# A reciprocal on another engine, an early tile for one set of matrices, and x loaded inside the gated unit: one step of a two-layer S5 and pooling backbone

## The chip, the core and the metric

The kernel runs on one core of a Trainium2 chip. The metric is the device time of one execution in microseconds (us). The core has five engines that run beside each other and wait for one another by semaphores: TensorE (PE in the rows; PEld is its weight load), VectorE (DVE), ScalarE (ACT), GpSimd (POOL) and SyncE (SP), which here does nothing but issue DMA transfers. ACT and POOL issue some transfers too. Each engine works off its own instructions strictly in the order in which they stand, so an instruction that waits holds up all that stands behind it.

## The reference

Two token streams go through the same two layers: a context of 128 tokens and a latent grid of 1024 tokens, both 1024 wide, in fp32. A layer is a token mixer, a LayerNorm, a SwiGLU of inner width 2816 and a second LayerNorm, each with modulation vectors that come from a conditioning vector. Layer 0 mixes with a bidirectional state-space scan, layer 1 by pooling over windows. Cut to layer 0, where the change lies:

```
def s5_mixer(h, ...):
    u = h.reshape(bsz, seq_len, 64, 16)
    y = u * d_skip
    for d in range(2):                       # forward, backward
        s_re, s_im, f_re, f_im = s5_scan(u, ..., reverse=(d == 1))
        y = y + (einsum(s_re, c_re[d]) - einsum(s_im, c_im[d]))
    y = gelu(y.reshape(bsz, seq_len, D_MODEL))
    val, gate = split(y @ glu_w + glu_b, 2)  # the gated unit
    return val * sigmoid(gate), ...

oc, fin_re, fin_im = s5_mixer(hc, ..., zeros, zeros)                 # context
ol, _, _ = s5_mixer(hl, ..., state_ssm_re, state_ssm_im)             # latents
xc = layer_norm(ALPHA * xc + g1c * oc, ...)
xl = layer_norm(ALPHA * xl + g1l * ol, ...)
fc = swiglu(modulate(xc, sh2c, sc2c), w_gate[i], w_up[i], w_down[i])
fl = swiglu(modulate(xl, sh2l, sc2l), w_gate[i], w_up[i], w_down[i])
```

`layer_norm` subtracts the mean over the 1024 channels and multiplies by `rsqrt(var + 1e-5)`.

## The kernel before

The scan is cut into chunks of 8 tokens: 128 chunks of the latents, 16 of the context. Within a chunk everything is a matrix product, between the chunks a recurrence is stepped.

**Tables (0 to about 176 us).** `ssm` loads parameters, and for each of eight blocks of 128 channels (`kt`, 8 groups of 16 channels) `ssm_u` transposes the input into `u`, `ssm_in` and `ssm_v` make the chunk inputs of the scan, `Z[0]` (forward) and `Z[1]` (backward), and `ssm_tables` makes two sets of matrices and writes them to DRAM: `kd[kt]` (the in-chunk matrices) and `mo[kt]` (from state to output, 1 MB). The adaLN weights (`adaw`) are loaded and multiplied beside it.

**Scan.** `scan_step` (lines 477 and 482) takes one chunk of both directions forward on VectorE: two products into `stt`, four sums into `Z`. First 15 steps for the context, then 127 for the latents (`ssm_scan_lat`).

**Context output.** `ssm_y_ctx` multiplies, for each `kt`, `u` by `mk` (L645) and the states by `mo` (L648), both loaded by `load_mo` (L589: eight pieces of `kd`, and L595: `mo`), applies a gelu and transposes (L659) into `xmc`. `load_mo` keeps the last four `mk` (4 buffers) and the last two `mo` (2 buffers). Then `ctx0a` runs the context's gated unit (`glu`, weights in `raw`) and its LayerNorm (`ln`), while the latent scan runs. With `scanning` set, `elem` gives GpSimd for the context's elementwise work; `ln_stats` takes the square root on ScalarE (L981), `nc.vector.reciprocal` on VectorE (L982) and refines the result by one Newton step (`stt`, on GpSimd here).

**Latent output.** `ssm_y` copies the states of a `kt` into `sd` (L626 ACT, L628 POOL, L630 DVE; 3 buffers), multiplies by `mk` and `mo` (L674, L677), applies a gelu on ScalarE (`yl`, L680) and writes `yd[kt]` to DRAM by POOL (L683). The order is 6, 7, 4, 5, 0, 1, 2, 3, so that `mk` of 4 to 7 and `mo` of 6 and 7 are still there. Beside it run the first 15 of the 22 steps of the context's SwiGLU (`ctx0b`, `ffn` L841): each is two weights of 0.5 MB through `raw`, which has three buffers for all users, and PE products into `psc`, which has two.

**Gated unit of the latents.** `yd` is read back as `yr` (L1187, two buffers, issued by POOL) and split by ScalarE and VectorE into a high and a low part (`xm`, `xn`, L821 and L822). `load_x` brings x in eight tiles of 128 tokens (`xr`, through `raw`), transposes them on PE (`px`, L421) and copies them on ScalarE (L422). Then `glu` runs for the first half A and the second half B of the latents; each of 8 values of `m` takes two weights through `raw`, split into `wh` and `wl`, and 48 products of 128x512. The remaining steps of the context's SwiGLU run between them with weights in `rc`.

After that both halves go through the SwiGLU, and layer 1 follows.

**What sets the order.** Every instruction is recorded in program order, and `TileContext(schedule_with_timeline_sim=True)` lets a scheduler put each engine's instructions, and the DMAs of each queue, in an order of its own, by durations that it assumes. So a change of one line can move instructions at many places. Buffers of a pool are handed on in turn; a transfer into a buffer waits on its queue until the last reader is through.

Of the kernel before, what the change touches and what calls it, by code (L numbers as in the profile page):

```python
# [41 lines left out]
class Kernel:  # L42
# [366 lines left out]

    def load_x(self):  # L410

        nc = self.nc
        xs = self.I["x_sample"].rearrange("o n d -> (o n) d")
        for q in range(8):
            xp = self.raw.tile([128, 1024], F32, tag="raw", name=f"xr{q}")
# [114 lines left out]
    def ssm_tables(self, tmp, kt, si):  # L530
# [50 lines left out]
        nc.scalar.dma_start(self.kd[kt].rearrange("g h m -> (g h) m"), ks.rearrange("p j h -> p (j h)"))  # L581

    def load_mo(self, tmp, kt):


        if kt not in self.mks[-4:]:
            m = tmp.tile([128, 8, 128], F32, tag="mk", name="mk", bufs=4)
            for s in range(8):
                self.nc.sync.dma_start(m[16 * s:16 * s + 16],  # L589
                                       self.kd[kt].rearrange("g h m -> h g m")[:, :, 16 * s:16 * s + 128])  # L590
            self.mks.append(kt)
            self.held["m", kt] = m
        if kt not in self.mos[-2:]:
            mo = tmp.tile([128, 2048], F32, tag="mo", name="mo", bufs=2)
            self.nc.sync.dma_start(mo, self.mo[kt])  # L595
            self.mos.append(kt)
            self.held["o", kt] = mo
        return (self.held["m", kt],
                self.held["o", kt].rearrange("p (d x g m) -> p d x g m", d=2, x=2, g=4))
# [88 lines left out]
    def ssm(self):  # L688
# [8 lines left out]
        with R("sst") as tmp:  # L697
            with R("ad0", "left") as ad:
                arow = self.ssm_params(pp, tmp, ad)
            self.ssm_modvec(pp, tmp, arow)  # L700
            self.ssm_dskip(pp, tmp)
        self.u = left.enter_context(R("ssmu", "left")).tile([128, G, NCH], F32, name="u")
        self.adp = self.rawc = None
# [4 lines left out]
        with R("ssu") as tmp:  # L708
            for kt in range(KT):
# [5 lines left out]
                for d in range(2):  # L715
                    self.ssm_in(si, d, kt, 4)
                self.ssm_tables(so, kt, si)
            while self.late:
                self.ssm_v()
# [8 lines left out]
        with R("ssy") as tmp:  # L728
            self.mks, self.mos, self.held = [], [], {}
            self.scanning = True  # L730
# [9 lines left out]
            self.ssm_scan_lat()  # L740
            for kt in (6, 7, 4, 5, 0, 1, 2, 3):
                self.ssm_y(tmp, kt)
# [141 lines left out]

    def glu(self, b, x, fill=iter(()), vx=lambda a: a, vs=lambda a: a):
        nc, I = self.nc, self.I
        gw = I["ssm_glu_w"][0].rearrange("(k p) m -> p k m", p=128)
        for m in range(8):
# [3 lines left out]
            nc.scalar.activation(sg, pg, AF.Sigmoid, bias=self.glu_b[:, 1, m:m + 1])  # L892
            self.stt(b, sg, pv, self.glu_b[:, 0, m:m + 1], sg, OP.add, OP.mult, self.glu_b[:, 0, m:m + 1])
            self.stt(b, vx(b.x[:, m, :]), vs(sg), self.gate[0, 0][:, b.i, m:m + 1], vx(b.x[:, m, :]),
                     OP.mult, OP.add)
# [59 lines left out]
    def ln_stats(self, b):  # L955
# [25 lines left out]
        nc.scalar.activation(q, pv, AF.Sqrt, bias=self.eps if b.split else self.epsc[:, 0:1])  # L981
        nc.vector.reciprocal(r, q)  # L982
        self.stt(b, q, pv, LN_EPS / (ALPHA * ALPHA), r, OP.add, OP.mult, self.epsc[:, 0:1])
# [163 lines left out]
    def build(self):  # L1147
        tc, nc = self.tc, self.nc
        with ExitStack() as st:
# [16 lines left out]
            self.gate, self.lnm = {}, {}  # L1166
            self.scanning = False
            self.ident = self.cp.tile([128, 128], F32, name="ident")
            make_identity(nc, self.ident)
# [11 lines left out]
            with tc.tile_pool(name="xm1", bufs=1) as xmp:  # L1181
                xm = [xmp.tile([128, 8, 512], F32R, name=f"xm{q}") for q in range(2)]
                with tc.tile_pool(name="glup", bufs=1) as tmp:
                    xm2 = [tmp.tile([128, 8, 512], F32R, name=f"xn{q}") for q in range(2)]
                    for k in range(8):
# [4 lines left out]
                        for q, x in enumerate((xm, xm2)):  # L1190
                            self.split_into(tok(x[0]), tok(x[1]), yv[:, ::-1, 64 * q:64 * q + 64])
                    self.load_x()
                    with tc.tile_pool(name="rawc", bufs=1) as self.rawc:
                        self.glu(A, xm, fill)
                        self.glu(B, xm2, fill)
# [120 lines left out]
```

## Time and profile before

| | us |
|---|---|
| median of 3 runs (2436.50 to 2446.79) | 2441.52 |
| the profiled execution | 2435.49 |
| its span, first to last instruction | 2433.7 |
| PE busy in it | 2243.9 (92%) |
| DVE busy | 1274.6 (52%) |
| ACT busy | 926.1 (38%) |
| POOL busy | 267.2 (11%) |

A row of the profile names the source line, the engine, the operation and the tiles (written tile first, buffer numbers left out), with partitions x elements. Times in the timeline views count from the first instruction. The span is 1.8 us shorter than the execution's own time. A step of the program order ("ffn", say) often stands in the trace as two records, since an fp32 product takes two passes. DMA shares are the mean busy share of 16 DMA engines.

### The profile page before, as it was taken

The page shows a single profiled execution, that of the slowest core. Times are in us where ns is not written, and L with a number is a line of the kernel's source. Part 1 is how long each engine was busy: PE and PEld are TensorE (multiplying, and loading weights), DVE is VectorE, ACT ScalarE, POOL GpSimd, SP SyncE. Part 2 cuts the span into 40 slices and gives each one's busy share as a digit, 9 for nine tenths or more (in the row PEclk, how much of TensorE's full clock was granted, in tenths as well). Part 3 has the DMA queues.
Part 4 walks back from the last instruction along what each step waited for, and adds up shares of the span by engine and source line. Part 5 has one row for each costly group of instructions (what it writes and reads, how often), then busy time and mean ns, then how long its engine had stood idle before and what let it go on. Part 6 is the DMA issues. An engine that isn't in the chain of part 4 may idle for free.

```text
span 2433.7 us, 33343 instructions
## 1 busy us (share of the span) xinstructions
PE 2243.9 (92%) x13105; PEld 1874.0 (77%) x13105; DVE 1274.6 (52%) x2421; ACT 926.1 (38%) x1377; POOL 267.2 (11%) x337
## 2 busy tenths in 40 slices
PE   4886768699999999999999999889999999999996
PEld 2655768588887777788888888777788888888996
DVE  6779684254546222456322775778422456422476
ACT  3763225343225222544322543226322443322464
POOL 4931236300010000100000010002000100000000
PEclk7995889799999999999999999999999999999998
DMA  7877559754554554423333225764333223333452
GB/s 226 247 236 199 156 150 271 207 156 145 160 166 153 160 187 160 169 96 95 96 99 100 96 96 161 231 193 135 104 100 99 96 95 96 95 96 100 143 200 104
DMA packets 458012, 357.22 MB, mean 147 GB/s; under 512 B 14960, under 2 KB 405888, under 8 KB 455808
## 3 DMA queue, kind: packets, MB, share of 16 engines
q1 hardware_dynamic: 451920, 340.91, 46.6%
q0 software_dynamic: 3200, 8.39, 1.2%
q10 hardware_dynamic: 2736, 5.80, 0.6%
q8 instruction: 103, 1.69, 0.3%
q14 instruction: 53, 0.43, 0.1%
HBM read 336.58 MB, written 18.35 MB: 146 GB/s over the span
## 4 chain that ended last, share of the span: by engine, by line
PE 79%; DMA 13%; DVE 3%; issue 2%; ACT 2%; POOL 1%; SPq 1%; ACTq 0%; DVEq 0%; POOLq 0%
PE ffn L837 13%; PE ffn L839 13%; PE ffn L838 13%; PE dn L838 6%; PE dn L837 6%; PE dn L839 6%; PE ffn L841 3%; PE dn L841 3%; DMA adaw<-ada_w 2%; PE glu L838 2%; PE glu L839 2%; PE glu L837 2%; DMA raw<-ffn_w_gate 2%; DMA raw<-ffn_w_down 1%; DMA raw<-ssm_glu_w 1%
## 5 line engine op out<-in xcount | busy, mean ns | idle before, releaser
L821 ACT ACTIVATE wh<-raw 128x1024 fp32r<-128x1024 f32 (+1 forms) x326 | 342.1, 1050 | 936.6 <-PE ffn L838 613.0
L822 DVE TENSOR_TENSOR wl<-raw,wh 128x1024 fp32r<-128x1024 f32 (+1 forms) x326 | 394.7, 1211 | 512.2 <-ACT wh L821 504.8
L838 PE MATMUL dn<-hkl,wh 128*128 128x512 f32 (+1 forms) x880 | 304.5, 348 | 0.3 <-DVE hkl L822 0.3
L839 PE MATMUL dn<-hkh,wl 128*128 128x512 f32 (+1 forms) x880 | 303.0, 347 | 0.0
L837 PE MATMUL ffn<-xp,wh 128*128 128x512 f32 x704 | 274.9, 391 | 2.2 <-ACT wh L821 2.2
L837 PE MATMUL ffn<-xm,wh 128*128 128x512 f32 x704 | 274.4, 391 | 1.3 <-ACT xm L821 0.7
L839 PE MATMUL ffn<-xp,wl 128*128 128x512 f32 x704 | 275.2, 391 | 0.2 <-DVE wl L822 0.2
L839 PE MATMUL ffn<-xm,wl 128*128 128x512 f32 x704 | 274.8, 391 | 0.0
L838 PE MATMUL ffn<-xm,wh 128*128 128x512 f32 x704 | 274.8, 390 | 0.0
L838 PE MATMUL ffn<-xp,wh 128*128 128x512 f32 x704 | 274.6, 391 | 0.0
L837 PE MATMUL dn<-hkh,wh 128*128 128x512 f32 (+1 forms) x880 | 262.5, 348 | 0.9 <-ACT hkh L821 0.9
L910 DVE TENSOR_TENSOR h<-ffn,sg 128x512 f32<-128x512 f32 x88 | 60.7, 689 | 245.2 <-PE ffn L839 245.1
L838 PEld LDWEIGHTS dn<-hkl,wh 128*128 128x128 f32 x880 | 166.6, 189 | 21.0 <-DVE hkl L822 0.5
L839 PEld LDWEIGHTS dn<-hkh,wl 128*128 128x128 f32 x880 | 166.5, 189 | 20.5
L837 PEld LDWEIGHTS dn<-hkh,wh 128*128 128x128 f32 x880 | 163.3, 189 | 23.3 <-ACT hkh L821 1.7
L841 PE MATMUL ffn<-xmc,raw 128*128 128x128 f32 x1184 | 149.6, 282 | 31.0 <-DMA raw<-ffn_w_gate 10.3
L841 PEld LDWEIGHTS ffn<-xmc,raw 128*128 128x128 f32 x1184 | 141.9, 196 | 40.3 <-DMA raw<-ffn_w_up 11.1
L837 PEld LDWEIGHTS ffn<-xm,wh 128*128 128x128 f32 x704 | 132.1, 188 | 33.1 <-issue 3.8
L837 PEld LDWEIGHTS ffn<-xp,wh 128*128 128x128 f32 x704 | 132.5, 188 | 30.4 <-ACT wh L821 2.5
L839 PEld LDWEIGHTS ffn<-xp,wl 128*128 128x128 f32 x704 | 132.5, 188 | 29.0 <-DVE wl L822 0.9
L839 PEld LDWEIGHTS ffn<-xm,wl 128*128 128x128 f32 x704 | 132.2, 188 | 29.0 <-issue 1.5
L838 PEld LDWEIGHTS ffn<-xp,wh 128*128 128x128 f32 x704 | 132.5, 188 | 28.1 <-issue 0.5
(331 smaller groups left out, 3308.0 us busy)
## 6 DMA issues: line engine op xcount, KB each, us to landing
raw<-ffn_w_down SPq DMA_DIRECT2D x126, 512.0 KB
raw<-ffn_w_gate SPq DMA_DIRECT2D x125, 512.0 KB
raw<-ffn_w_up SPq DMA_DIRECT2D x125, 512.0 KB
adaw<-ada_w SPq DMA_DIRECT2D x96, 512.0 KB
raw<-ssm_glu_w SPq DMA_DIRECT2D x48, 512.0 KB
mo<-mo SPq DMA_DIRECT2D x14, 1024.0 KB
rc<-ffn_w_down SPq DMA_DIRECT2D x40, 256.0 KB
mo<-otab SPq DMA_DIRECT2D x32, 256.0 KB
```

What stands on the lines that cost most here:

```text
L821: nc.scalar.activation(h, src, AF.Copy)
L822: nc.vector.tensor_tensor(l, src, h.bitcast(F32), op=OP.subtract)
L837: nc.tensor.matmul(ps, wh, xh, start=start, stop=False)
L838: nc.tensor.matmul(ps, wh, xl, start=False, stop=False)
L839: nc.tensor.matmul(ps, wl, xh, start=False, stop=stop)
L841: nc.tensor.matmul(ps, w[0], x[0], start=start, stop=stop)
L910: v.tensor_tensor(h[:, f, :], self.in_sb(b, v, pu), sg, op=OP.mult)
```

## The change

Four edits. `ln_stats` takes the reciprocal on the engine that `elem` gives: on VectorE as before, on GpSimd as a power with exponent -1, read from a new one-column tile `minus`. This concerns the context's first LayerNorm alone, the only one that runs with `scanning` set. `mk0`, the in-chunk matrices of block 0, gets a tile of its own, loaded while the tables of block 3 are made; the ring of `mk` has three buffers instead of four, and the latent blocks come in the order 6, 7, 5, 0, 1, 2, 3, 4. `load_x` takes a list of tiles and is called inside `glu` of half A, for tiles 0 to 3 at `m = 0` and for 4 to 7 at `m = 3`, instead of ahead of it. The memset of `minus` is added at the start.

```diff
--- before.py
+++ after.py
@@ -407,11 +407,11 @@
                 nc.scalar.activation(self.XC.rearrange("p k (c t) -> p t k c", t=8)[:, 4 * half + t4],
                                      px[:, 128 * t4:128 * t4 + 128].rearrange("p (k c) -> p k c", c=16), AF.Copy)
 
-    def load_x(self):
+    def load_x(self, qs):
 
         nc = self.nc
         xs = self.I["x_sample"].rearrange("o n d -> (o n) d")
-        for q in range(8):
+        for q in qs:
             xp = self.raw.tile([128, 1024], F32, tag="raw", name=f"xr{q}")
             nc.sync.dma_start(xp, xs[128 * q:128 * q + 128, :])
             for kh in range(2):
@@ -580,14 +580,17 @@
                                            kp[po, 224 + 16 * gp:240 + 16 * gp], op0=OP.mult, op1=OP.add)
         nc.scalar.dma_start(self.kd[kt].rearrange("g h m -> (g h) m"), ks.rearrange("p j h -> p (j h)"))
 
+    def load_mk(self, m, kt):
+        for s in range(8):
+            self.nc.sync.dma_start(m[16 * s:16 * s + 16],
+                                   self.kd[kt].rearrange("g h m -> h g m")[:, :, 16 * s:16 * s + 128])
+
     def load_mo(self, tmp, kt):
 
 
-        if kt not in self.mks[-4:]:
-            m = tmp.tile([128, 8, 128], F32, tag="mk", name="mk", bufs=4)
-            for s in range(8):
-                self.nc.sync.dma_start(m[16 * s:16 * s + 16],
-                                       self.kd[kt].rearrange("g h m -> h g m")[:, :, 16 * s:16 * s + 128])
+        if kt not in self.mks[-3:] and kt:
+            m = tmp.tile([128, 8, 128], F32, tag="mk", name="mk", bufs=3)
+            self.load_mk(m, kt)
             self.mks.append(kt)
             self.held["m", kt] = m
         if kt not in self.mos[-2:]:
@@ -699,6 +702,8 @@
                 arow = self.ssm_params(pp, tmp, ad)
             self.ssm_modvec(pp, tmp, arow)
             self.ssm_dskip(pp, tmp)
+        mk0 = left.enter_context(R("ssmk", "left")).tile([128, 8, 128], F32, name="mk0")
+        self.held = {("m", 0): mk0}
         self.u = left.enter_context(R("ssmu", "left")).tile([128, G, NCH], F32, name="u")
         self.adp = self.rawc = None
         self.Z = []
@@ -715,6 +720,8 @@
                 for d in range(2):
                     self.ssm_in(si, d, kt, 4)
                 self.ssm_tables(so, kt, si)
+                if kt == 3:
+                    self.load_mk(mk0, 0)
             while self.late:
                 self.ssm_v()
         self.ssm_scan_ctx(si)
@@ -726,7 +733,7 @@
         self.open_ctx(cblk)
         self.open_hc(cblk)
         with R("ssy") as tmp:
-            self.mks, self.mos, self.held = [], [], {}
+            self.mks, self.mos = [], []
             self.scanning = True
             self.yb = [tmp.tile([128, 8, 8, 16], F32, tag="yl", name=f"yb{q}", bufs=2) for q in range(2)]
             for q in range(2):
@@ -738,7 +745,7 @@
             self.drain(fill)
             self.ctx0a()
             self.ssm_scan_lat()
-            for kt in (6, 7, 4, 5, 0, 1, 2, 3):
+            for kt in (6, 7, 5, 0, 1, 2, 3, 4):
                 self.ssm_y(tmp, kt)
         left.close()
         self.cright = right
@@ -882,7 +889,7 @@
             v.tensor_scalar(t, x, s, None, op0=op0)
         v.tensor_tensor(out, t, y, op=op1)
 
-    def glu(self, b, x, fill=iter(()), vx=lambda a: a, vs=lambda a: a):
+    def glu(self, b, x, fill=iter(()), vx=lambda a: a, vs=lambda a: a, hooks={}):
         nc, I = self.nc, self.I
         gw = I["ssm_glu_w"][0].rearrange("(k p) m -> p k m", p=128)
         for m in range(8):
@@ -891,6 +898,7 @@
             sg = b.tmp.tile([128, b.n], F32, tag="sg" + b.tg, name="sg", bufs=2)
             nc.scalar.activation(sg, pg, AF.Sigmoid, bias=self.glu_b[:, 1, m:m + 1])
             self.stt(b, sg, pv, self.glu_b[:, 0, m:m + 1], sg, OP.add, OP.mult, self.glu_b[:, 0, m:m + 1])
+            self.load_x(hooks.get(m, ()))
             self.stt(b, vx(b.x[:, m, :]), vs(sg), self.gate[0, 0][:, b.i, m:m + 1], vx(b.x[:, m, :]),
                      OP.mult, OP.add)
             next(fill, None)
@@ -979,7 +987,10 @@
         r = b.tmp.tile([128, n], F32, tag="lr" + b.tg, name="lr", bufs=1)
         q = b.tmp.tile([128, n], F32, tag="lq" + b.tg, name="lq", bufs=1)
         nc.scalar.activation(q, pv, AF.Sqrt, bias=self.eps if b.split else self.epsc[:, 0:1])
-        nc.vector.reciprocal(r, q)
+        if v is nc.vector:
+            v.reciprocal(r, q)
+        else:
+            v.tensor_tensor(r, q, self.minus.to_broadcast([128, n]), op=OP.pow)
         self.stt(b, q, pv, LN_EPS / (ALPHA * ALPHA), r, OP.add, OP.mult, self.epsc[:, 0:1])
         self.stt(b, q, q, -0.5, r, OP.mult, OP.mult)
         self.stt(b, r, q, 1.5, r, OP.add, OP.mult)
@@ -1165,6 +1176,8 @@
             self.XC = P("xcres").tile([128, 8, 128], F32, name="XC")
             self.gate, self.lnm = {}, {}
             self.scanning = False
+            self.minus = self.cp.tile([128, 1], F32, name="minus")
+            nc.vector.memset(self.minus, -1.0)
             self.ident = self.cp.tile([128, 128], F32, name="ident")
             make_identity(nc, self.ident)
             self.ssm()
@@ -1189,9 +1202,8 @@
                         tok = lambda a: a[:, k].rearrange("p (c t) -> p t c", t=8)
                         for q, x in enumerate((xm, xm2)):
                             self.split_into(tok(x[0]), tok(x[1]), yv[:, ::-1, 64 * q:64 * q + 64])
-                    self.load_x()
                     with tc.tile_pool(name="rawc", bufs=1) as self.rawc:
-                        self.glu(A, xm, fill)
+                        self.glu(A, xm, fill, hooks={0: range(4), 3: range(4, 8)})
                         self.glu(B, xm2, fill)
                         self.drain(fill)
                     self.rawc = None
```

The scheduler moves much more than that. Three places follow; first before, then after. (Line numbers grow by up to 13.)

On DVE, in the middle of the latent scan, the reciprocal stood between two sums of one scan step (`stt` and `Z` are the two directions' tiles, `lr` and `lq` the LayerNorm's):

```order
L477 TENSOR_TENSOR stt_364<-rm,Z_566 128x128
L482 TENSOR_TENSOR Z_562<-stt_363,Z_562 128x64
L482 TENSOR_TENSOR Z_566<-stt_364,Z_566 128x64
L482 TENSOR_TENSOR Z_562<-stt_363,Z_562 128x64
L982 RECIPROCAL lr<-lq 128x128
L482 TENSOR_TENSOR Z_566<-stt_364,Z_566 128x64
L477 TENSOR_TENSOR stt_363<-rm,Z_562 128x128
```

Now it stands on POOL between the sum of squares and the Newton step of the same LayerNorm, and DVE has nothing but scan steps there:

```order
L984 TENSOR_TENSOR sq<-sq 128x256 x3
L985 TENSOR_TENSOR sq<-sq 128x128
L993 TENSOR_TENSOR lr<-lq,minus 128x128
L890 TENSOR_TENSOR lq<-st,lr 128x128
L889 TENSOR_SCALAR st<-lq 128x128
L890 TENSOR_TENSOR lq<-st,lr 128x128
L889 TENSOR_SCALAR st<-lq 128x128
L890 TENSOR_TENSOR lr<-st,lr 128x128
```

The instruction has gone from one in-order engine to another, and stays at its place in the LayerNorm's chain.

On SP, at the end of the latent blocks, where x and the first weights of the gated unit are loaded (`xr` x, `mo` a block's state matrices, `mk` its in-chunk matrices):

```order
L589 DMA mk<-kd_97 16x8x128 x7
L416 DMA xr_4828<-x_sample 128x1024
L416 DMA xr_4842<-x_sample 128x1024
L416 DMA xr_4856<-x_sample 128x1024
L595 DMA mo<-mo_88 128x2048
L595 DMA mo<-mo_89 128x2048
L416 DMA xr_4870<-x_sample 128x1024
L416 DMA xr_4884<-x_sample 128x1024
L416 DMA xr_4898<-x_sample 128x1024
L416 DMA xr_4912<-x_sample 128x1024
L416 DMA xr_4926<-x_sample 128x1024
L830 DMA raw<-ssm_glu_w 128x8x128 x5
```

Now:

```order
L598 DMA mo<-mo_90 128x2048
L837 DMA raw<-ffn_w_gate 128x8x128
L837 DMA raw<-ffn_w_up 128x8x128
L837 DMA raw<-ffn_w_gate 128x8x128
L837 DMA raw<-ffn_w_up 128x8x128
L837 DMA raw<-ssm_glu_w 128x8x128 x2
L416 DMA xr_4902<-x_sample 128x1024
L416 DMA xr_4916<-x_sample 128x1024
L416 DMA xr_4930<-x_sample 128x1024
L1294 DMA rc<-ffn_w_gate 128x4x128 x2
L1294 DMA rc<-ffn_w_up 128x4x128 x2
L1294 DMA rc<-ffn_w_gate 128x4x128 x2
```

The loads of x stand behind the first two weights of the gated unit, and the context's last weights of these 15 steps behind the last `mo`: before, the first `mo` of the latent blocks stood behind 22 of the 30 `raw` weights, now behind 9, and the last one behind 26.

On DVE, at the end of the scan (`hc` is the product that ends a step of the context's SwiGLU, `sd` the copies of a latent block):

```order
L477 TENSOR_TENSOR stt_363<-rm,Z_562 128x128
L910 TENSOR_TENSOR hc<-ffn,sg 128x128
L477 TENSOR_TENSOR stt_364<-rm,Z_566 128x128
L482 TENSOR_TENSOR Z_562<-stt_363,Z_562 128x64
L482 TENSOR_TENSOR Z_566<-stt_364,Z_566 128x64
L482 TENSOR_TENSOR Z_562<-stt_363,Z_562 128x64
L482 TENSOR_TENSOR Z_566<-stt_364,Z_566 128x64
L630 COPY sd<-Z_562 64x512
```

Now:

```order
L477 TENSOR_TENSOR stt_366<-rm,Z_572 128x128
L477 TENSOR_TENSOR stt_365<-rm,Z_568 128x128
L482 TENSOR_TENSOR Z_572<-stt_366,Z_572 128x64
L482 TENSOR_TENSOR Z_568<-stt_365,Z_568 128x64
L482 TENSOR_TENSOR Z_572<-stt_366,Z_572 128x64
L482 TENSOR_TENSOR Z_568<-stt_365,Z_568 128x64
L477 TENSOR_TENSOR stt_366<-rm,Z_572 128x128
L633 COPY sd<-Z_568 64x512
```

The products `hc` that stood inside the scan are gone from it; the first one on DVE now stands behind the copies of four latent blocks.

## Rows read from the trace of the kernel before

**Rows 1.** Busy time by stretch: us, PE, PEld, DVE, ACT, POOL, PEclk, DMA share, GB/s.
```profile
197.60:284.10 86.50, 69.05 (x644) 60.46 (x645) 86.49 (x517) 30.09 (x101) 14.11 (x33) 0.69 0.59 164
284.10:311.10 27.00, 13.42 (x101) 11.94 (x100) 0.00 (x0) 6.18 (x16) 14.19 (x24) 0.85 0.53 151
312.00:323.00 11.00, 4.13 (x19) 4.13 (x20) 11.00 (x46) 3.62 (x8) 10.17 (x17) 0.50 0.01 1
323.00:350.70 27.70, 22.93 (x190) 21.75 (x189) 27.70 (x167) 4.30 (x14) 3.15 (x6) 0.99 0.74 210
318.87:449.90 131.03, 110.33 (x868) 106.49 (x869) 74.54 (x251) 52.44 (x74) 62.50 (x85) 0.93 0.78 219
449.90:505.40 55.50, 36.85 (x208) 31.14 (x206) 20.78 (x21) 30.52 (x39) 8.48 (x16) 0.85 0.77 238
505.40:717.00 211.60, 211.60 (x1178) 183.64 (x1177) 89.32 (x102) 65.02 (x70) 1.68 (x1) 1.00 0.51 148
```

**Rows 2.** Timeline of DVE: start us, us, engine, line, operation, tiles [idle before <-releaser].
```profile
193.35 0.19 DVE L167 TENSOR_TENSOR mod<-adat,adab 128x32 f32<-128x32 f32 x1 [3.18 <-PE adat L166]
...
311.12 0.95 DVE L982 RECIPROCAL lr<-lq 128x128 f32<-128x128 f32 x1 [27.03 <-ACT lq L981]
...
354.04 0.29 DVE L910 TENSOR_TENSOR hc<-ffn,sg 128x128 f32<-128x128 f32 x1 [3.03 <-ACT sg L908]
...
361.32 4.38 DVE L630 COPY sd<-Z 64x512 f32<-64x512 f32 x4
```

**Rows 3.** Timeline of PE, 190 to 320 us and 340 us.
```profile
191.64 1.08 PE L648 MATMUL pyc<-mo,Z 128*16 128x128 f32 x16 [2.38 <-DMA mo<-mo]
...
221.82 1.22 PE L841 MATMUL glu<-xmc,raw 128*128 128x128 f32 x4 [4.60 <-DMA raw<-ssm_glu_w]
...
318.87 7.74 PE L841 MATMUL ffn<-xmc,raw 128*128 128x128 f32 x48 [8.25 <-POOL xmc L1003]
...
340.03 4.01 PE L841 MATMUL ffn<-xmc,raw 128*128 128x128 f32 x32 [0.45 <-ACT sg L908]
```

**Rows 4.** The DMA issues of SP in order of time, 180 to 433 us.
```profile
180.21 5.59 SPq L589 DMA_DIRECT2D mk<-kd  x8
185.84 0.43 SPq L595 DMA_DIRECT2D mo<-mo  x1
...
418.83 13.72 SPq L595 DMA_DIRECT2D mo<-mo  x2
```

**Rows 5.** Groups of POOL, 170 to 330 us: us in all, mean ns | idle before.
```profile
L882 POOL TENSOR_SCALAR st<-sg,gate 128x128 f32<-128x128 f32 x8 | 5.1, 632 | 0.8
...
L883 POOL TENSOR_TENSOR lq<-st,lr 128x128 f32<-128x128 f32 x2 | 1.0, 500 | 2.5 <-DVE Z L482 2.5
```

**Rows 6.** Timeline of PE, 426 to 480 us.
```profile
426.73 0.77 PE L677 MATMUL py<-sd,mo 128*128 128x128 f32 x2 [3.09 <-DMA mo<-mo]
...
449.68 0.61 PE L677 MATMUL py<-sd,mo 128*128 128x128 f32 x4
450.66 3.10 PE L421 MATMUL px<-ident,xr 128*128 128x128 f32 x24 [0.38 <-ACT X L422]
...
475.66 5.15 PE L841 MATMUL ffn<-xmc,rc 128*128 128x128 f32 x24 [12.84 <-DMA rc<-ffn_w_gate]
```

**Rows 7.** Timeline of ACT, 450 to 505 us.
```profile
450.01 2.07 ACT L422 ACTIVATE X<-px 128x512 f32<-128x512 f32 x4 [2.67 <-PE py L674]
451.94 0.63 ACT L680 ACTIVATE yl<-py 128x512 f32<-128x512 f32 x1
...
483.99 0.28 ACT L908 ACTIVATE sg<-ffn 128x128 f32<-128x128 f32 x1 [7.92 <-PE ffn L841]
...
503.97 1.25 ACT L821 ACTIVATE xn<-yr 128x512 fp32r<-128x512 f32 x1
```

**Rows 8.** Timeline of POOL, 452 to 464 us.
```profile
452.86 4.18 POOL L683 DMA_DIRECT2D yd<-yl  x8 [6.88 <-ACT yl L680]
463.31 1.12 POOL L1187 DMA_DIRECT2D yr<-yd  x2 [6.27 <-DMA raw<-ssm_glu_w]
```

## The prediction

> **What bounds the kernel now.** I read the busy time by stretch first. From 505.4 us on PE has no gap: in the stretch to 717 us it is busy for 211.60 of 211.60 us [rows 1], and the order of the instructions behind that is nearly untouched by the change. So the change is worth what it shifts that point, less what it adds to PE's work behind it. Ahead of it PE has gaps, and the timelines of the engines say what they are.
>
> Two chains run side by side from about 200 us on. The scan of the latents keeps DVE busy for 86.49 of 86.50 us up to 284.1 us; then DVE does nothing for 27 us [rows 1], because the reciprocal of the context's LayerNorm stands in the middle of the scan and waits 27.03 us for ScalarE's square root [rows 2]. The scan goes on afterwards, is held once more for 3.03 us by a product of the context's SwiGLU, and ends at 361.3 us, where the copies of the first latent block begin [rows 2]. The other chain is the context: its LayerNorm is through at 318.87 us, where PE begins the SwiGLU [rows 3]. The reader is to see that the context chain is the slower one at 311 us and that one instruction ties the scan to it.
>
> From 318.87 to 449.9 us PE does the context's 15 SwiGLU steps and the eight latent blocks: 110.33 us busy in 131.03, at a mean clock of 0.93, with the DMA engines at a share of 0.78 and 219 GB/s [rows 1]. The last blocks wait for `mo` one by one: two loads stand on SP from 418.83 us for 13.72 us [rows 4], and PE waits 3.09 us for one of them [rows 6]. From the last product of a latent block (449.68 us [rows 6]) to the last split part (503.97 + 1.25 = 505.2 us [rows 7]) the end is set by the way through DRAM: `yd` written at 452.86 us, `yr` asked for at 463.31 us [rows 8], and a stall in which PE waits 12.84 us for the first `rc` weight [rows 6] and ScalarE 7.92 us for PE [rows 7] while splits stand behind it.
>
> **The change part by part.** The sum is made against the profiled execution, 2435.5 us (a span of 2433.7 and 1.8 around it, which the change does not touch), which is 6.0 us below the median of 2441.5; the shift is then applied to the median. 0.5% of it is 12.2 us, about what can be told from no change.
>
> *The scan.* The wait of 27.03 us and the 0.95 us of the reciprocal go; the `hc` product with its 3.03 + 0.29 us goes out of the scan too [rows 2]. What is late next on DVE is the contention with POOL: with POOL busy 10.17 of 11.00 us the scan's instructions take 11.00 / 46 = 0.239 us, alone 86.49 / 517 = 0.167 us [rows 1]. The LayerNorm's 14.19 us of POOL work between 284.1 and 311.1 us now lie beside the scan, and 14.19 x (1 - 0.167 / 0.239) = 4.3 us are lost. The scan would end at 361.3 - 31.3 + 4.3 = 334.3 us.
>
> *The power on POOL.* The trace of before has no power. The nearest row is a two-operand product of the same 128x128 on POOL, 0.500 us [rows 5]; from above, the kernel's own exponential is 14 elementwise instructions, and a power of an exponential and a logarithm would be 28 passes, 14 us. I take 2 us, nearer to the row. It replaces 0.95 us and a second change of engine, so the context is 1 us later (from 0.5 earlier to 13 later). Behind it in POOL's queue stands the rest of this LayerNorm, for which PE's SwiGLU waits.
>
> *The tile mk0.* Ahead of the context's first output, SP issues eight pieces for block 0 (5.59 us) and then `mo` at 185.84 us, for which PE waits until 191.64 us [rows 3, 4]. Without the pieces `mo` is issued about 5.6 us earlier. The transpose of the adaLN vectors, which stands behind that product on PE, then no longer holds the scan for 3.18 us [rows 2]: 3.2 us for both chains. PE's wait of 4.60 us for a weight of the gated unit [rows 3] goes as well, because SP now has that weight ahead of the third `mo`. Together 7.8 us for the context. The eight pieces now stand in the table stage, where PE, DVE, ACT, POOL and DMA all are well filled: nothing if they are hidden, 5.6 us if SP is the limit; I take 2. The context's LayerNorm ends at 318.9 - 7.8 + 2 + 1 = 314 us (309 to 332), the scan at 334.3 - 3.2 + 2 = 333 us.
>
> *The latent blocks.* Their work and that of the 15 steps is the same, less 16 of the transposes of x, at 3.10 / 24 = 0.13 us each [rows 6]: 110.3 - 2.1 = 108 us, and about 106 with fewer waits, after which the clock is low. The new order interleaves 17 of the 30 weights with the six `mo`, where only 8 stood, so that the serial loads at the end are hidden by products. New waits: ScalarE has the first block's copies ahead of the first silu, so PE, with two buffers, does two steps (4.01 us each [rows 3]) from 314 us and then waits for the scan until about 329 us, 7 us. I keep 5 of the others. Last product at 314 + 106 + 12 = 432 us against 450.3: 18.3 us earlier. All 20.7 us of waits kept would make it 9.6.
>
> *To the last split part.* Before, 16 copies of x stood on ScalarE from 450.01 us on, four of them ahead of the last gelu, 2.07 us [rows 7]: gone. The `rc` weights stand behind three loads of x instead of five weights of the gated unit, and I give back half of the 7.92 us. Eight copies of x (0.5 to 0.6 us each) now stand between the splits, half of them in waits: 2.4 us. Sum: 4 us earlier, between 10 earlier and 4 later.
>
> *x inside the gated unit.* The second four tiles come where PE has no gap: 32 transposes x 0.13 = 4.1 us. They pass the ring of three `raw` buffers in which the next `m`'s weights come, and a slot is free only after ScalarE's copy. The fourth tile and the weight behind it are two transfers in a row, partly beside 16 matmuls of the context: 0 to 8 us, I take 2.5. Together 6.6 us later.
>
> Sum: -18.3 - 4 + 6.6 = -15.7, rounded to -16 us: 2419.5 as a profiled execution, **2425.5 us** as a median. The memset of a column is nothing beside the loads at the start.
>
> **The rivals.** *The gain is filled up* (2436 us). The stretch of the latent blocks is bounded by PE's work and the weights, not by the scan's end: PE is busy 110.33 of 131.03 us and the DMA share is 0.78 [rows 1]. If the waits come back to 20.7 us, 8.7 of the 16 go, and with the table stage 2 us longer the shift is -5. Against it: the waits that I see at the end are those of serial loads [rows 4, 6].
>
> *More is gained* (2411 us). Waits of 6 instead of 12, the whole 7.92 us of ScalarE, no stall in the ring: -16 - 6 - 4 - 2.5 = -28.5, with two more at the start. For it: half of the DMA engines is idle behind 505 us (share 0.51 [rows 1]).
>
> *The power is slow* (slower). Its price above 1 us comes one to one on the context, and PE's SwiGLU, the ring and the latent blocks behind stand in order behind it. At 18 us the gain is eaten; from 30 us on it is slower by over 0.5%; at 40 us it is 2441.5 - 16 + 38 = 2463. For it: a power is not one pass; POOL has no such row. Against it: 30 us would be 60 products of this size.
>
> *The first power pays once more* (2431.5 us). A one-off preparation of POOL ahead of its first power would fall on the same place, with its price added to the context alone. The rows speak against it in general: the first `st` products on POOL, a form that starts with the context's gated unit, take 632 ns on average over all eight, with 0.8 us of idle time ahead of all [rows 5]. By the Trainium skill, GPSIMD Engine Reference, section Instruction dispatch, the first call of a freshly loaded kernel pays about 6 us that no instruction in a profile shows; by that rule the shift would be -10 instead of -16. No row here shows such a gap, and nothing shows that a power needs a load.
>
> *The scan is held elsewhere.* The edit does move the wait off DVE in the order, and the only other foreign instructions in the scan are gone, so I give this nothing of its own.
>
> **How the numbers follow.** Forecast 0.52, filled up 0.18, more gained 0.17, one-off preparation 0.05, slow power 0.08. The forecast's own range is 2418 to 2433. About four fifths of its chance lie beyond 12.2 us: 0.42, with the 0.17 0.59 for faster; within 0.5% the rest of the forecast, the filled-up case and the one-off, 0.33; slower 0.08. The range of 8 in 10 takes in the larger gain and the filled-up case and leaves out the slow power: 2405 to 2440 us.
>
> **What would show it.** In the new profile: DVE without a gap from about 195 us to the scan's end, near 333; a POOL power of about 2 us; the first product of the context's SwiGLU near 314; the last product of a latent block near 432; the last split near 483; PE without a gap from there, but with 32 transposes and a short wait behind `m = 3`. I am wrong if the scan ends early and the last product of the latent blocks does not follow it, if the power takes over 10 us, or if PE waits more than 8 us in the gated unit.

## The result, and the profile after

The change makes the kernel slower: 2455.18 us (median of 9 runs, 2452.32 to 2460.30) against 2438.59 us (9 runs, 2430.62 to 2446.79), a ratio of 1.0072 [1.0053, 1.0092]. The forecast was 2425.5 us, 0.59 for faster and 0.08 for slower. The profiled execution has a span of 2457.3 us, 23.6 more than that of before.

Busy time by stretch in the kernel after, columns as in [rows 1]; the stretches are the scan, the two halves of its rest, the context's SwiGLU with the latent blocks, the way to the last split part, the gated unit, and last the up products of layer 1:
```profile
199.40:283.32 83.92, 70.48 (x699) 61.59 (x691) 83.92 (x494) 31.46 (x105) 17.53 (x40) 0.75 0.67 186
283.32:304.86 21.54, 7.45 (x52) 6.51 (x52) 21.54 (x91) 4.92 (x12) 11.95 (x19) 0.73 0.40 114
304.86:332.60 27.74, 0.01 (x1) 0.01 (x1) 27.68 (x151) 0.21 (x2) 27.23 (x12) 0.50 0.00 1
332.60:451.90 119.30, 104.08 (x854) 101.84 (x854) 40.12 (x57) 64.92 (x85) 60.38 (x85) 0.95 0.83 233
451.90:504.00 52.10, 35.20 (x195) 29.88 (x196) 21.75 (x21) 26.77 (x33) 8.48 (x16) 0.84 0.76 233
504.00:717.00 213.00, 210.70 (x1170) 182.87 (x1169) 87.04 (x96) 67.24 (x76) 1.67 (x1) 0.99 0.54 156
1671.20:2296.30 625.10, 622.40 (x2670) 502.17 (x2669) 260.66 (x282) 209.69 (x265) 13.60 (x11) 0.99 0.32 95
```
and the last of these stretches in the kernel before:
```profile
1663.60:2273.50 609.90, 607.47 (x2670) 500.81 (x2670) 260.43 (x282) 210.07 (x266) 13.92 (x11) 1.00 0.33 98
```
The hole in DVE is gone (27 idle us in [rows 1], none here), but from 304.86 to 332.60 us PE and the DMA engines stand still. And the 2670 product records of layer 1 take 625.1 us instead of 609.9, in a stretch that no edit touches: of PE's places in the order 39 differ, all among the first 178. The timelines of ACT and POOL show what PE stands for (the square root, the power, the product behind it):
```profile
304.42 0.37 ACT L989 ACTIVATE lq<-lnv,epsc 128x128 f32<-128x128 f32 x1 [1.40 <-PE lnv L960]
304.86 20.86 POOL L993 TENSOR_TENSOR lr<-lq,minus 128x128 f32<-128x128 f32 x1 [1.33 <-ACT lq L989]
325.80 0.49 POOL L890 TENSOR_TENSOR lq<-st,lr 128x128 f32<-128x128 f32 x1
```
The power takes 20.86 us; the product of the same size behind it 0.49 us. PE's rows that answer to [rows 3] and [rows 6] (first context output, first SwiGLU product, first and last product of a latent block with `mo`):
```profile
193.13 1.10 PE L651 MATMUL pyc<-mo,Z 128*16 128x128 f32 x16 [8.41 <-ACT Z L612]
...
332.60 7.94 PE L848 MATMUL ffn<-xmc,raw 128*128 128x128 f32 x48 [28.21 <-POOL xmc L1014]
340.37 0.39 PE L680 MATMUL py<-sd,mo 128*128 128x128 f32 x2
...
450.64 0.61 PE L680 MATMUL py<-sd,mo 128*128 128x128 f32 x4
```
and DVE's to [rows 2]:
```profile
194.87 0.19 DVE L167 TENSOR_TENSOR mod<-adat,adab 128x32 f32<-128x32 f32 x1
...
338.29 2.92 DVE L633 COPY sd<-Z 64x512 f32<-64x512 f32 x4
356.15 4.41 DVE L633 COPY sd<-Z 64x512 f32<-64x512 f32 x4 [14.95 <-PE py L680]
```
The adaLN vectors hold the scan no more (3.18 us in [rows 2]), and the scan ends at 338.3 us instead of 361.3. The last latent product nevertheless comes at 450.64 us, as before (449.68 in [rows 6]). For [rows 4], SP now issues the last single `mo` at 428.89 us; for [rows 7], the last split part:
```profile
501.47 1.23 ACT L828 ACTIVATE xn<-yr 128x512 fp32r<-128x512 f32 x1
```
Last, the groups of layer 1's up products on the two pages (busy us, mean ns | idle before), in the kernel after:
```profile
L844 PE MATMUL ffn<-xp,wh 128*128 128x512 f32 x704 | 280.3, 398 | 2.2 <-ACT wh L828 2.2
L846 PE MATMUL ffn<-xp,wl 128*128 128x512 f32 x704 | 280.0, 398 | 0.5 <-DVE wl L829 0.5
L845 PE MATMUL ffn<-xp,wh 128*128 128x512 f32 x704 | 279.9, 398 | 0.0
```
and before:
```profile
L837 PE MATMUL ffn<-xp,wh 128*128 128x512 f32 x704 | 274.9, 391 | 2.2 <-ACT wh L821 2.2
```
Layer 0's (`xm` in place of `xp`) stay at 391 and 390 ns in both. The granted clock is 1.00, the 2.4 GHz level, in the middle of the stretch in both kernels (0.99 and 1.00 over all of it).

### The profile page after: what moved, and what is told of

It reads as the page before. It is cut to its first block, busy times and chain, and to the rows that moved or that the text cites. A ratio compares the mean times of both kernels' runs of the same rounds, so it can differ in the third digit from the quotient of the medians.

```text
span 2457.3 us, 33344 instructions
## 1 busy us (share of the span) xinstructions
PE 2254.7 (92%) x13105; PEld 1871.8 (76%) x13105; DVE 1281.1 (52%) x2421; ACT 937.5 (38%) x1387; POOL 284.2 (12%) x338
## 4 chain that ended last, share of the span: by engine, by line
PE 80%; DMA 11%; DVE 3%; ACT 2%; POOL 2%; issue 1%; SPq 0%; ACTq 0%; POOLq 0%; DVEq 0%
PE ffn L844 13%; PE ffn L846 13%; PE ffn L845 13%; PE dn L844 6%; PE dn L845 6%; PE dn L846 6%; PE ffn L848 4%; PE dn L848 3%; PE glu L845 2%; PE glu L846 2%; PE glu L844 2%; DMA adaw<-ada_w 2%; DMA raw<-ffn_w_gate 2%; DMA raw<-ffn_w_down 1%; DMA mo<-mo 1%
## 5 line engine op out<-in xcount | busy, mean ns | idle before, releaser
L828 ACT ACTIVATE wh<-raw 128x1024 fp32r<-128x1024 f32 (+1 forms) x326 | 341.5, 1049 | 947.7 <-PE ffn L845 623.4
L844 PE MATMUL ffn<-xp,wh 128*128 128x512 f32 x704 | 280.3, 398 | 2.2 <-ACT wh L828 2.2
L845 PE MATMUL ffn<-xp,wh 128*128 128x512 f32 x704 | 279.9, 398 | 0.0
```

What stands on the lines that cost most here:

```text
L828: nc.scalar.activation(h, src, AF.Copy)
L844: nc.tensor.matmul(ps, wh, xh, start=start, stop=False)
L845: nc.tensor.matmul(ps, wh, xl, start=False, stop=False)
```

## The experiments

Three questions: why the products of layer 1 are slower, what the power costs, and why an earlier context and scan bring nothing. Times are medians, ratios are to the kernel before in the same session.

**The place in memory.** The new tile `minus` has 4 bytes in a partition and is given 32; it is the first tile on the left, so all that is allocated from the left lies 32 bytes further, the weights `wh` and `wl` among it. `xp`, the moving operand of layer 1's up products, lies on the right and stays. By the addresses of the compiled programs `xp0` lies 147,200 bytes above the first `wh` before, and 147,168 after. In the other split products (`xm`, `hk`) both operands move together.

*e1_wide*: distance 64 bytes less than before.
```
-            self.minus = self.cp.tile([128, 1], F32, name="minus")
+            self.minus = self.cp.tile([128, 16], F32, name="minus")
```


> The changed kernel with 16 columns instead of one for the tile of -1 (64 bytes of a partition instead of 32), of which the power reads one column: every operation and its order stay, only the pools behind that tile lie 32 bytes further. Theory of the place in memory: some 15 of the 16.6 us come from the weights of layer 1's SwiGLU, which the one-column tile puts 32 bytes off the step of 64 at which its moving operand stands; so the mean of an up product of layer 1 goes back from 398 to 391 ns, and the time to about 2440 us, within 5 us of the kernel before. Rival, that the order of the work or the power slows these products: 398 ns and 2455 us stay.


2452.29 us, 1.0052 [1.0035, 1.0069]; the median product of layer 1 takes 394 ns, after the change 396, before 389. That a distance of a multiple of 64 bytes is free is refuted, the rest open.

*e2_pad32*: the kernel before, 32 bytes less.
```
+            self.pad = self.cp.tile([128, 8], F32, name="pad")
+            nc.vector.memset(self.pad, 0.0)
             self.ident = self.cp.tile([128, 128], F32, name="ident")
```


> The kernel before, with an unused tile of 32 bytes of a partition ahead of the identity matrix and nothing else of the change. Theory of the place in memory: the up products of layer 1 go from 391 to 398 ns, 2112 of them, and the time rises by about 15 us, to 2454. Rival, that the slower products come from the order of the work: 391 ns and 2439 us, as without the tile.


2452.27 us, 1.0057 [1.0037, 1.0076], 396 ns. An unused tile alone does nearly all of the damage, with layer 1's instructions in the order of the kernel before.

*a1_noshift*: the change, with nothing moved.
```
-            self.minus = self.cp.tile([128, 1], F32, name="minus")
+            self.minus = self.epsc[:, 8:9]
```


> The changed kernel with its -1 in an unused column of the 24-column tile at the right edge instead of a tile of its own: same operations, same power, but no pool lies elsewhere than in the kernel before. Theory of the place in memory, now without the rule of 64 bytes that the wider tile refuted (any distance other than that of before would do): the up products of layer 1 go back from 398 to 391 ns and the time falls by some 15 us from the changed kernel's, to 2440. Rival, that the power or the order of the work slows them: 398 ns and 2455 us.


2440.03 us, 0.9988 [0.9975, 1.0002], 389 ns: the whole slowdown is gone, with the power still there, at 20.86 us in its trace too, and with layer 1's instructions in the order of the kernel after.

*p1_right32* (32 bytes less, by the right side), *p2_both* (128 less, both sides moved), *p3_pad128* (128 less) and *p4_pad256* (256 less), all from the kernel before:
```
p1:  -tile([128, 24], F32, name="epsc")   +tile([128, 32], F32, name="epsc")
p2:  pad of 8 columns as in e2, epsc of 48 columns
p3:  pad of 32 columns      p4:  pad of 64 columns
```


> The kernel before with 32 columns instead of 24 in the tile at the right edge: the pools on the right, with the moving operand of layer 1's up products, lie 32 bytes lower, and the weights where they lay. Theory that the distance between the two operands counts: up products of layer 1 at 398 ns, 2454 us. Rival, that only the weights' own place counts (they must lie on a step of 128 bytes): 391 ns and 2439 us. Layer 0's up products, whose operands both lie on the left, stay at 389 ns by both.

> The kernel before with the unused tile of 32 bytes on the left, which alone made it slower, and 48 instead of 24 columns at the right edge: the weights lie 32 bytes higher and the moving operand of layer 1's up products 96 lower, so that their distance is again a multiple of 128 bytes, but neither operand lies on one. Theory that the distance counts, in steps of 128 bytes: 391 ns, 2439 us. Rival, that each operand must lie on a step of its own: 398 ns or more and 2454 us or more.

> The kernel before with an unused tile of 128 bytes instead of 32 on the left. Theory that steps of 128 bytes count: 391 ns and 2439 us. Rival, that any shift at all, or a larger step, counts: 394 to 398 ns and 2450 to 2454 us.

> The kernel before with an unused tile of 256 bytes on the left. By 32 bytes of distance the up products of layer 1 took 396 ns, by 64 bytes 394, by 128 bytes 393, against 389. Theory of steps of 256 bytes: 389 ns again and 2440 us. Rival, that only a distance of a still larger step or the old one alone is free: 391 to 393 ns and 2446 to 2452 us.

| | distance | median ns | first to last up product of layer 1, us | ratio to before |
|---|---|---|---|---|
| before | 147,200 | 389 | 610.1 | 1 |
| p4_pad256 | -256 | 389 | 610.8 | 0.9997 [0.9981, 1.0012] |
| p3_pad128 | -128 | 393 | 622.4 | 1.0024 [1.0009, 1.0039] |
| p2_both | -128 | 393 | 623.4 | 1.0051 [1.0031, 1.0071] |
| e1_wide | -64 | 394 | 623.8 | 1.0052 [1.0035, 1.0069] |
| p1_right32 | -32 | 396 | 624.0 | 1.0058 [1.0041, 1.0075] |
| e2_pad32 | -32 | 396 | 624.1 | 1.0057 [1.0037, 1.0076] |
| after | -32 | 396 | 625.3 | 1.0072 [1.0053, 1.0092] |

p1 moves only the right side and is as slow as e2, so the weights' own place is not it; the median is the same for the same distance, whichever side moved. The step from 393 to 396 ns is one of the medians; the means are 396 to 398 ns at all three distances (391 before). p2 and p3 refuted my step of 128 bytes. With 256 the price is gone: 147,200 is 575 times 256, and `xm`, whose products take 389 ns in the median in all these kernels, lies 90,112 bytes above the first `wh` in all of them, 352 times 256. Kernels with the distance of before, these and the ones below, need 610 to 613 us for layer 1. What in the chip makes the distance count (two reads that meet, or a read and a write) no run here shows.

**The power.** *e3_dve* (the reciprocal back on VectorE, no `minus`):
```
-        if v is nc.vector:
-            v.reciprocal(r, q)
-        else:
-            v.tensor_tensor(r, q, self.minus.to_broadcast([128, n]), op=OP.pow)
+        nc.vector.reciprocal(r, q)
```


> The changed kernel with the reciprocal back on VectorE and without the tile of -1, so that the matrices' own tile and the x inside the gated unit stand alone and the pools lie where they lay before. Theory (power and place in memory are the two causes): products of layer 1 at 391 ns; the context's LayerNorm ends near 313 us instead of 332.6, VectorE idles some 16 to 21 us in the scan again, the scan ends near 355, the last split part near 500; with 6 us more in the gated unit the time is 2438 to 2445 us, 10 to 17 below the changed kernel. Rival (the matrices' own tile and the x in the gated unit are what costs): it stays near 2455.


2436.91 us, 0.9978 [0.9964, 0.9992]. The SwiGLU begins at 318.1 us, the last latent product at 455.0. The rival, that the own tile and x inside are what costs, falls; without the power and without the shift the rest of the change is a small gain.

*f3_arsqrt* (`q` for GpSimd's branch is not computed; VectorE's keeps its square root):
```
-            v.tensor_tensor(r, q, self.minus.to_broadcast([128, n]), op=OP.pow)
+            nc.scalar.activation(r, pv, AF.Abs_reciprocal_sqrt, bias=self.epsc[:, 0:1])
```


> The changed kernel with the context's square root and power replaced by one inverse square root on ScalarE (the Newton step behind it stays), without the tile of -1: nothing of this LayerNorm is left on VectorE, and GpSimd has no power. Theory: the 20.86 us of the power were what ate the gain on the context's path and the place in memory the rest, so PE begins the context's SwiGLU near 311 us, the scan ends by 340, the last latent block's product comes 12 to 18 us before 450, and the time is 2420 to 2432 us, faster than the kernel before. Rival, that the latent blocks are bounded by the weights and matrices that are loaded, not by this path: last product still near 448, and 2438 to 2445 us.


2432.75 us, 0.9975 [0.9964, 0.9986]: with e3 the best of the kernels that compute everything, faster than both given ones, but not the 2420 to 2432 of the theory. The SwiGLU begins at 315.9 us, yet the last latent product starts at 449.2. An `hc` product in the scan held DVE:
```profile
351.34 0.29 DVE L918 TENSOR_TENSOR hc<-ffn,sg 128x128 f32<-128x128 f32 x1 [15.82 <-ACT sg L916]
```

*k4_halves* (a1 with the power in two):
```
-            v.tensor_tensor(r, q, self.minus.to_broadcast([128, n]), op=OP.pow)
+            for c in range(0, n, n // 2):
+                v.tensor_tensor(r[:, c:c + n // 2], q[:, c:c + n // 2], self.minus.to_broadcast([128, n // 2]), op=OP.pow)
```


> The changed kernel with nothing moved in memory and the power as two instructions of 64 columns. If its price goes by the column (20.86 us / 128 = 163 ns): 10.4 us each, 20.9 together. If it is paid once, for the first power of the program: the first one stays near 20 us and the second is a fraction of it. If it is paid by the instruction: two of some 20 us, 41 together.


The powers' line in its trace (min/median/max ns, first and last start):
```profile
L994 POOL TENSOR_TENSOR lr<-lq,epsc x2: 10677/10704/10732, 305.8 to 316.5; 128x64 f32<-128x64 f32 x2
```
Two equal halves: a price by the column, 163 to 168 ns each. The dearer one is so by 0.06 us, so the rival of a first power that pays once more is out.

**The latent blocks.** *h1_scanfree* is f3 with eight instead of six `hc` products on GpSimd, *h2_xahead* is h1 with x loaded ahead again, *h3_freeonly* the kernel before with f3's and h1's edits alone:
```
h1:  -            v = self.elem(b, f < 6)
     +            v = self.elem(b, f < 8)
h2:  +                    self.load_x(range(8))      (ahead of the pool rawc)
     -  self.glu(A, xm, fill, hooks={0: range(4), 3: range(4, 8)})
     +  self.glu(A, xm, fill)
```


> The changed kernel as the prediction took it: the power of 20.86 us is replaced by ScalarE's inverse square root, the first eight of the context's hc products go to GpSimd instead of the first six, so that none stands on VectorE inside the scan (one held it for 15.8 us with the inverse square root alone), and no pool lies elsewhere. Theory of the prediction, that the latent blocks follow the scan's end: scan through at 338 us, PE begins the context's SwiGLU at 315, last product of a latent block at 432 to 438, time 2422 to 2428 us. Rival, that loads bound these blocks (two tiles each for the matrices, so that their loads wait for the products of the block before): last product at 445 to 452 whatever the scan does, and 2433 to 2440 us.

> The same kernel, with x loaded ahead of the gated unit again, as before the change. Theory: the 32 transposes and the wait in the ring that the x inside the unit costs (4.1 and 2.5 us in the prediction) are won back, the gated unit's stretch on PE is 6 us shorter and the time 4 to 7 us below the kernel with x inside. Rival: ahead of the unit the copies of x stand on ScalarE and SP before the last split parts again, so the unit begins as much later and the time is the same within 2 us.

> The kernel before with nothing but the scan set free: inverse square root on ScalarE, eight hc products on GpSimd, old order of the blocks, no tile of its own for the first matrices, x ahead of the gated unit. Theory that the scan's end sets the end of the latent blocks: their last product 10 us or more ahead of 450, 2425 to 2432 us. Rival, that it doesn't: last product near 448 and 2436 to 2442 us, no change to the kernel before.


2439.41, 2437.14 and 2438.89 us; 0.9988 [0.9973, 1.0004], 0.9990 [0.9975, 1.0004], 0.9993 [0.9975, 1.0011]: no change, three times. In h1 the scan is through at 341.2 us and the SwiGLU begins at 317.08, but its last latent product starts at 453.8. What PE waited for in h1 from 316 to 452 us (us in all, times, longest):
```profile
PE py L680 <- DMA mo<-mo: 8.7, 3, 4.9
PE ffn L848 <- POOL xmc L1014: 7.4, 1, 7.4
PE py L680 <- DVE sd L633: 5.5, 4, 2.0
PE ffn L848 <- DMA raw<-ffn_w_gate: 5.2, 5, 2.4
PE ffn L848 <- DMA raw<-ffn_w_up: 3.7, 5, 2.0
PE py L677 <- DMA mk<-kd: 2.2, 1, 2.2
```
Loads make up 19.8 us of it (8.7 + 5.2 + 3.7 + 2.2). Its stretches of 338 to 452 us (columns as above):
```profile
338.00:360.00 22.00, 19.00 (x156) 17.80 (x156) 5.95 (x15) 6.33 (x14) 5.59 (x8) 1.00 0.80 232
360.00:420.00 60.00, 53.23 (x437) 52.18 (x437) 19.49 (x23) 26.32 (x33) 29.84 (x40) 0.94 0.88 247
420.00:452.00 32.00, 19.56 (x126) 18.37 (x125) 11.55 (x11) 7.72 (x11) 20.15 (x28) 0.79 0.53 141
```
and two of them before:
```profile
360.00:420.00 60.00, 53.66 (x453) 52.44 (x451) 26.84 (x34) 34.19 (x40) 34.67 (x43) 0.97 0.95 271
420.00:452.00 32.00, 23.68 (x159) 22.27 (x160) 10.26 (x10) 8.48 (x14) 19.67 (x29) 0.84 0.55 150
```
Where the weights and the `mo` matrices are loaded together, the DMA engines are busy for 0.88 to 0.95 of the time; behind that, at 0.53 to 0.55, PE waits for single loads, with two `mo` tiles that come free block by block.

The kernel after loads the same, and does not have this end. Its second stretch, and PE's waits for loads from 332.6 to 451.9 us, 14.1 us in all:
```profile
420.00:452.00 32.00, 29.00 (x242) 28.48 (x240) 8.87 (x13) 17.88 (x22) 13.85 (x19) 0.95 0.85 244
PE py L680 <- DMA mo<-mo: 5.3, 3, 2.1
PE ffn L848 <- DMA raw<-ffn_w_gate: 4.7, 3, 2.0
PE ffn L848 <- DMA raw<-ffn_w_up: 3.2, 2, 1.6
PE py L677 <- DMA mk<-kd: 0.9, 1, 0.9
```
The order differs. In the four kernels with the power (after, e1, a1, k4) the six `mo` stand on SP behind 9, 11, 14, 18, 22 and 26 of the 30 weights. In those without it (e3, f3, h1, h2) the first stands behind 22 and the last three behind all 30, as in the kernel before.

Two kernels without these six loads (k2 from h1, k5 from the kernel before; their output is not the reference's, PE's products are all there):
```
-        if kt not in self.mos[-2:]:
+        if len(self.mos) < KT and kt not in self.mos[-2:]:
     (and the block uses one of the last two tiles that were loaded)
```


> The kernel with the scan free (h1) without six of the eight loads of mo: the first two blocks' matrices are used for all eight, so the latents' output is another one; PE's products are all there. Theory that the loads bound the latent blocks (the DMA engines at a share of 0.88 to 0.95 from 360 to 420 us, single loads waited for behind it): the blocks' last product falls from 453.8 us to 425 to 435, PE waits for mo no more, and the time to 2415 to 2425 us. Rival, that the way from product to copy to product within a block bounds them: last product at 445 or later, over 2432 us.

> The kernel before without the same six loads, scan and reciprocal as they are (the latents' output is another one again). If the loads alone bound the blocks, it gains as much as the kernel with the scan free does, 15 to 20 us, and their last product comes at 430 to 436 us. If the scan's end is the second bound behind them, it gains less: the first latent block can't begin before 360 us, last product at 438 to 445, 2426 to 2434 us, and the two kernels without the loads differ by some 10 us.


k2: 2426.75 us, 0.9931 [0.9904, 0.9958]. Its latent products (min/median/max ns, first and last start):
```profile
L680 PE MATMUL py<-sd,mo x256: 275/275/422, 352.9 to 433.2; 128*128 128x128 f32 x128
```
In k5, 2431.87 us, 0.9957 [0.9942, 0.9972], the last one starts at 438.5. So in the order of the kernel before these loads are a bound: without them even the kernel with the held scan gains 10 us, and h1 some 13. Between k2 and k5, the free scan and the rest of the change, lie some 6 us (0.0026 of 2440), not the 10 that I expected, and as the two intervals overlap, this difference is not shown. No run here tests the loads, or a cheap power, in the order of the kernel after. k2's time is above its theory: from its last latent product to the end of the gated unit it takes 279.0 us, where the other kernels with x inside take 270.9 to 276.7.

## Why the prediction was wrong

- **"The memset of a column is nothing beside the loads at the start."** This is the step that failed for the sign. I priced the tile by its memset and not by what it moves. It costs 15.2 us in layer 1 (625.3 - 610.1 in the table; 14 in e2 and p1 at the same distance), of 16.6 in the medians; a1 against the change gives it back. "The order of the instructions behind is nearly untouched" held, and was not enough: the same instructions were slower. No rival of mine had a place in memory in it.
- **The power on POOL, 2 us (0.5 to 14).** This is the step that failed for the size: it left nothing of the gain. The power takes 20.86 us; the truth lay above my upper bound, which I had built from an exponential and a logarithm of the kernel's own. The excess of 18.9 us goes through the whole chain: the SwiGLU began at 332.6 us where I had 314, and the last latent product ended at 451.3 where I had 432. From the start of the scan to the end of the gated unit both kernels take some 549 us: 8.8 more up to the SwiGLU, 12.7 less from there to the last latent product, 4 more behind it. The rival of a slow power was right on the price and on the place. By its own sum a power of 21 us is a loss of 3, and a1 is at 0.9988 [0.9975, 1.0002], between a gain of 6 and none: that sum was too high by 2 to 9 us. But e3, f3 and h1 show that taking the power out does not bring the forecast's gain either, for the reason that follows.
- **The latent blocks, 18.3 us earlier.** In the kernel after the stretch from the first SwiGLU product to the end of the last latent one is 118.7 us long, against the 118 that I gave. The size is right, in part by luck: 7 us of mine were a wait for the scan, which ended ahead of PE's first product with `mo` (338.3 and 340.4 us), and PE waited 14.1 us for loads in place of the 5 us of other waits that I kept. And it hangs on an order that the planner wrote with the power in it: 48 product records of the SwiGLU stand ahead of the first product with `mo`, and the stretch takes 117 to 119 us in all four kernels with the power. In e3, f3, h1 and h2, without it, 256 to 272 records stand there, the `mo` loads come as late as in the kernel before, and the stretch takes 133 to 141 us; in h1, with the context early and the scan free as I wanted it, 137 (317.1 to 454.0). There the rival "the gain is filled up" is right, and stronger than I made it: not 8.7 of 16 us but, in h1 and h2, all that can be told from none (e3 and f3 keep 5 or 6). I had read the share of 0.78 [rows 1] as a mean; within it stand 60 us at 0.95. Whether an early context in the order of the kernel after would have ended at 432 stays open: no kernel here has both.
- **The tile mk0, 7.8 us for the context.** The waits went as forecast (DVE 3.18, PE 4.60 us), though PE's first context output now waits 8.41 us for ACT, not for `mo`. From the scan's start to the SwiGLU e3 needs 139.4 us, before 146.2: 6.8 won. The eight pieces in the table stage (2 us) can't be told from the spread: the scan starts at 172.7 to 179.1 us in the eight profiled kernels without `mk0`, at 175.2 to 181.2 in the nine with it. The profile of [rows 3] has the earliest of these starts.
- **To the last split part, 4 us earlier; x in the gated unit, 6.6 later.** Together +2.6. From the last latent product to the end of the gated unit it is 270.4 to 272.5 us in nine kernels with x ahead (mean 271.5), and 270.9 to 276.7 with x inside (mean 273.0 without k2): +1.5. Right in sign, smaller in size; h1 and h2, which differ by this alone, are not told apart.
- **What stays open.** Of the 23.6 us between the two profiles 15.2 are in layer 1, 4.9 in the start of the scan, within its spread. From the gated unit to the pool stage's split products it is 840.7 us after and 837.3 before; a1 and k4 have 840 too, e1 and e3 838. I have no cause for these 2 to 3 us.

## What to carry to other kernels

A new tile has the price of what it moves: before a small tile is put ahead of others, look which operands of one instruction lie in pools on different sides, and keep their distance. Before a wait is costed as a gain, cut the stretch behind it into pieces, look for those where the DMA engines are nearly full, and see where the loads stand in the planner's order: with all loads in place the same products took 117 to 119 us in one order here and 127 to 141 in the other, and taking out the slow instruction changed the order with it.

## What the runs showed of the hardware

- 128x512 products of a split float32 operand took 389 ns in the median (a cadence of 222 in 50 us) when moving operand and weights lay a multiple of 256 bytes apart (three distances: 147,200, 146,944 and 90,112), 393 at 128, 394 at 64 and 396 at 32 bytes off it (216 in 50 us), at a granted clock of 1.00 in these 50 us. The Trainium skill, SBUF — State Buffer, section Operand start alignment, says only at which addresses an operand may start and that its runs timed nothing; no run here contradicts it, and the price is beside it.
- A power of 128x128 float32 on GpSimd took 20.86 us, where a product of this size took 0.49 us. The Trainium skill, GPSIMD Engine Reference, section Instruction dispatch, has about 6 us for the first call of a freshly loaded kernel; here the first power started 0.07 us after ScalarE's square root (304.42 + 0.37 to 304.86), and its two halves cost 10.68 and 10.73 us, so no such price shows.
